# How far ahead the experts' weight tiles are requested: 43 instead of 34 before the experts' stage, 38 instead of 34 within it

## The chip, the cores and the metric

The kernel runs on one core of one Trainium2 chip. The metric is the device time of one execution in microseconds (us). The engines are PE (matrix products, with PEld for the loads of its weights), DVE and ACT (elementwise work), POOL (elementwise work and the indirect DMAs) and SP, which issues nearly all plain DMAs in one queue, strictly in order. All DMAs share 16 DMA engines.

## The reference, cut to what matters

The program is one decoder block over 1024 tokens of width 1024: adaLN modulation, a projection to q, k and v, eight heads of dilated window attention and eight of stick-breaking attention, the output projection with the residual, and then a mixture of 32 SwiGLU experts, of which each token takes two of one group of eight. The part around the change is the mixture:

```
order = jnp.argsort(expert)
...
buf = jnp.zeros((cap, d), h.dtype).at[dest].set(h[tok_sorted])
...
return (jax.nn.silu(xb @ w_gate[e]) * (xb @ w_up[e])) @ w_down[e]
...
contrib = y[dest] * w_sorted[:, None].astype(y.dtype)
return jnp.zeros((n, d), y.dtype).at[tok_sorted].add(contrib)
```

After it come the second residual and a last RMSNorm. All is float32. An expert's weights are 6 MB (1024x512 for the gate, the same for the up projection, 512x1024 down), so 32 experts bring 201 MB through the DMA engines.

## The kernel before, in words

**Slots.** All large tiles (inputs, scores, weights, intermediate results) live in one pool `u` of `NSLOT = 49` slots of 128 partitions x 4 KB. A new tile takes a slot that an earlier tile has given back in the order of the program; if the earlier tile's last reader or writer, a DMA among them, is not done when the new tile is first written, the writer waits. Which slot a tile gets is settled when the program is built.

**Order.** The whole program is unrolled and every engine runs its instructions in the order in which they were recorded. In the attention's last pair of heads the recorded order weaves three strands together: the attention itself, the output projection with the residual (`out_mm`), and the routing (`route0` to `route3`), tile of 128 tokens by tile. Into this the requests for the experts' weights are spread by `load_to(n)`, which requests weight tiles until `n` have been requested in all:

```
def spread(us, mark, to):
    m = len(us) - mark
    for j in range(m, 0, -1):
        us.insert(mark + j, p0(lambda c=held[0] + (to - held[0]) * j // m: load_to(c)))
    held[0] = to
```

`LDS` gives the number reached after each of the eight token tiles (and two steps behind them). Such a request waits for the ACT instruction recorded just before it, and from the 15th on for the landing of the request 14 before (`PACE`). The requests stand in SP's queue between the loads of `x` (L118, `x<-acc`) and its stores (L936, `x1d<-x`), on which the routing and the gathers rest.

**The experts' stage.** Twelve tiles of 512 KB make an expert's weights: `ew_0` to `ew_7` for gate and up, `ew_8` to `ew_11` for down. Ahead of each product the loop requests more, so that the requests stand `LL` tiles beyond the product:

```
if kind in "GD":
    load_to(max(loaded[0], wpos[o] + LL - wpos[o] * LT // len(wseq)))
```

Each expert e goes through these steps: POOL gathers its tokens' rows into `xe` (L1222), ACT scales them (L1233), PE transposes them into `xp` (L1255) and ACT and DVE write `xs`; PE multiplies by the gate and up tiles into `gu` (L1266, L1273); ACT and DVE make `act`; PE transposes it into `ap` (L1306) and ACT copies that into the tile `at` (L1308, step T); PE multiplies `at` by the down tiles into `y` (step D); ACT and DVE make `ys` (step Y), and POOL adds its rows into `acc` in DRAM by an indirect DMA (L1339), called the scatter here. The tile `ys` can give its slot to another only when its scatter has landed. Experts 0 to 4 and the even ones above hold up to 96 tokens, the odd ones from 5 on 64, so from expert 4 on the work repeats in pairs of one large and one small expert, with 24 weight tiles each. Recorded order around a step T: the first four or five gate and up products of the next expert, T, one more of these products, then D and Y of the expert, then the rest of the next one's. Tile `xs`, `act`, `sg`, `at`, `yt` and `ys` take their slots from the same pool as the weights.

Of the kernel before, what the change touches and what calls it, by code (L numbers as in the profile page):

```python
# [38 lines left out]
RP, RU = 6, 0  # L39
PO = 1  # L40
PO2 = 22
LDS = [6, 6, 11, 14, 18, 22, 28, 33, 33, 34]
PACE = 14
TZ, DZ = 2, 3
NG, NP = 12, 3
# [14 lines left out]
QS = "AS"  # L60
TAIL = "s3 s4 s5 r0-3 o0 y o1 g3-6 o2 s6 s7 x o3 o4 g6-9 o5 o6 o7 o8"
XA, TA, DA = 6, 4, 5
LLX = 34
LT = 0
NT = 0
PLO = ()
# [30 lines left out]
def build(nc, tc, I, out, cap=CAP):  # L97
# [944 lines left out]

    LOADS = LDS

# [176 lines left out]
    def load_x(e):  # L1221
        g = G.indirect_dma_start(out=XE[e % 3][:capof(e)], out_offset=None, in_=x1d[:],  # L1222
                                 in_offset=bass.IndirectOffsetOnAxis(ap=listof(e), axis=0),
                                 bounds_check=T - 1, oob_is_err=False)
        if e == 1:
            after[0] = g.ins
# [146 lines left out]

    LL = LLX
    load_x(0)
# [209 lines left out]
```

## Time and profile before

| | us |
|---|---|
| median of 3 runs | 1330.21 (1327.76 to 1332.28) |
| profiled execution, its own time | 1326.88 |
| its span, first to last instruction | 1325.1 |
| PE busy in the span | 1161.6 |
| first product of the experts' stage | 741.8 |
| last `at` copy (expert 31) | 1278.9 |

The profiled execution is 3.3 us below the median, and 1.8 us of it lie outside the span. The page's busy shares are averages over stages that are limited by different things: up to 740 us PE and DVE alternate, and the DMA engines have idle time; from 740 us on they are nearly always busy. So the experts' stage is read by itself, by its rhythm: the time from one small expert's `at` copy to the next small expert's, which covers one pair.

### The profile page before, as it was taken

The numbers are of one execution on the slowest core, as the hardware profiler recorded it, in microseconds if no ns is written. First come the engines' busy times: TensorE is split into PE (matmuls) and PEld (weight loads), VectorE is DVE, ScalarE is ACT, GpSimd is POOL, SyncE is SP. The second block draws the span as 40 slices with busy tenths as digits, with TensorE's granted clock in tenths as the row PEclk, the third lists the DMA queues.
The fourth block names the chain that finished last, engine by engine and source line by source line (L and its number), as shares of the span: only waits on it lengthen the run. The fifth ranks groups of instructions, "written<-read, shape, count | busy, mean of one in ns | idle before, by whom it ended". The sixth has DMA issues, their size and how long they took to land.

```text
span 1325.1 us, 19365 instructions
## 1 busy us (share of the span) xinstructions
PE 1161.6 (88%) x6800; PEld 685.0 (52%) x6800; DVE 736.3 (56%) x1418; ACT 531.2 (40%) x1079; POOL 239.7 (18%) x306
## 2 busy tenths in 40 slices
PE   4699999999999999699887999899999998899960
PEld 3497778778866887477666422232332222222310
DVE  6958773865497848978866243333333333333324
ACT  5246553656555435434534432332222222222212
POOL 3600010110100002322323111111111111111203
PEclk9799999999999999899999899999999999999985
DMA  9423443431001010356667899999999999999984
GB/s 354 166 67 97 155 149 105 145 74 55 22 27 48 17 65 0 132 209 237 244 223 260 301 319 363 358 384 376 374 373 377 370 376 378 377 380 391 361 287 196
DMA packets 89384, 304.54 MB, mean 230 GB/s; under 512 B 12417, under 2 KB 14849, under 8 KB 89282
## 3 DMA queue, kind: packets, MB, share of 16 engines
q1 hardware_dynamic: 81778, 282.00, 57.6%
q0 software_dynamic: 6352, 17.05, 5.4%
q10 hardware_dynamic: 1152, 4.19, 0.8%
q8 instruction: 56, 0.92, 0.3%
q14 instruction: 46, 0.38, 0.1%
HBM read 278.30 MB, written 29.63 MB: 232 GB/s over the span
## 4 chain that ended last, share of the span: by engine, by line
PE 44%; DVE 22%; DMA 19%; ACT 8%; issue 4%; POOL 2%; SPq 0%; POOLq 0%; DVEq 0%; ACTq 0%
DMA ew<-we 16%; PE y L1266 5%; PE gu L1266 5%; PE o L573 4%; DVE K L532 3%; DVE wada L210 2%; PE tp L549 2%; PE op L666 2%; PE op L668 2%; PE op L667 2%; PE y L1273 2%; DVE P L514 2%; PE gu L1273 2%; PE pv L460 2%; PE pj L417 2%
## 5 line engine op out<-in xcount | busy, mean ns | idle before, releaser
L1266 PE MATMUL gu<-ew,xs 128*64 128x512 f32 x1024 | 249.0, 606 | 9.2 <-DMA ew<-we 5.7
L1324 DVE TENSOR_TENSOR ys<-y,bc_gate 64x512 f32<-64x512 f32 x64 | 44.0, 688 | 215.3 <-PE y L1273 128.5
L1266 PEld LDWEIGHTS gu<-ew,xs 128*64 128x64 f32 x1024 | 63.2, 136 | 142.7 <-issue 78.1
L1266 PE MATMUL y<-ew,at 128*64 128x512 f32 x512 | 124.4, 614 | 11.1 <-DMA ew<-we 8.8
L1243 ACT ACTIVATE xs<-xp,modc,affn 128x96 f32<-128x96 f32 (+1 forms) x128 | 51.6, 418 | 155.0 <-PE xp L1255 92.7
L1339 POOL DMA_INDIRECT acc<-ys,lsP x27 | 38.7, 1434 | 372.8 <-DVE ys L1330 230.8
L549 PE MATMUL tp<-ident,P 128*128 128x128 f32 x576 | 88.5, 279 | 18.9 <-DVE P L533 11.2
L532 DVE TENSOR_TENSOR_SCAN K<-K 128x1024 f32<-128x1024 f32 (+7 forms) x64 | 92.9, 1451 | 5.9 <-ACT K L520 5.7
L516 ACT ACTIVATE P<-P,st 128x1024 f32<-128x1024 f32 (+7 forms) x64 | 49.8, 778 | 87.9 <-DVE st L529 45.4
L549 PEld LDWEIGHTS tp<-ident,P 128*128 128x128 f32 x576 | 65.5, 141 | 37.1 <-DVE P L533 9.7
L573 PE MATMUL o<-PT,v 128*64 128x256 f32 (+1 forms) x640 | 75.5, 375 | 9.4 <-DVE PT L554 5.8
L1266 PEld LDWEIGHTS y<-ew,at 128*64 128x64 f32 x512 | 34.8, 138 | 93.5 <-issue 41.8
L1241 DVE TENSOR_SCALAR xs<-xp,affn,modc 128x96 f32<-128x96 f32 (+1 forms) x128 | 45.4, 363 | 61.1 <-ACT xs L1243 56.7
L520 ACT ACTIVATE K<-S 128x1024 f32<-128x1024 f32 (+7 forms) x64 | 41.8, 653 | 71.4 <-PE S L503 34.1
L210 DVE CUSTOM_DVE_ANT_0 wada<-wada,sc 128x1024 f32<-128x1024 f32 x48 | 64.4, 1353 | 9.7 <-DMA wada<-w_adaT 9.6
L1273 PE MATMUL gu<-ew,xs 128*32 128x512 f32 x576 | 69.3, 598 | 0.0
L514 DVE CUSTOM_DVE_ANT_0 P<-S,B 128x1024 f32<-128x1024 f32 (+7 forms) x64 | 48.3, 755 | 35.8 <-PE S L501 32.9
L1278 ACT ACTIVATE yt<-y 64x512 f32<-64x512 f32 x18 | 10.7, 593 | 141.4 <-PE xp L1255 119.6
L573 PEld LDWEIGHTS o<-PT,v 128*64 128x64 f32 x640 | 46.2, 141 | 39.4 <-DVE PT L554 8.3
L552 ACT ACTIVATE PT<-tp 128x512 f32<-128x512 f32 (+3 forms) x120 | 56.0, 494 | 14.9 <-PE tp L549 14.0
L533 DVE TENSOR_TENSOR P<-P,K 128x1023 f32<-128x1023 f32 (+7 forms) x64 | 51.6, 806 | 5.7 <-ACT P L521 0.7
L554 DVE COPY PT<-tp 128x512 f32<-128x512 f32 (+3 forms) x72 | 37.3, 537 | 16.1 <-PE tp L549 15.7
(632 smaller groups left out, 2510.4 us busy)
## 6 DMA issues: line engine op xcount, KB each, us to landing
ew<-we SPq DMA_DIRECT2D x384, 512.0 KB
wada<-w_adaT SPq DMA_DIRECT2D x48, 512.0 KB
wqk<-wqk SPq DMA_DIRECT2D x16, 512.0 KB
xT<-xT SPq DMA_DIRECT2D x16, 256.0 KB
wv<-wv SPq DMA_DIRECT2D x8, 512.0 KB
B<-bias SPq DMA_DIRECT2D x8, 512.0 KB
wo<-w_out SPq DMA_DIRECT2D x8, 512.0 KB
x<-x SPq DMA_DIRECT2D x8, 512.0 KB
```

Of the source, the lines that this page charges most:

```text
L210: V.tensor_tensor_reduce(w, w, sc, op0=ALU.mult, op1=ALU.add, scale=1.0, scalar=0.0, accum_out=modc[:, v * 8 + k:v * 8 + k + 1])
L514: V.tensor_tensor_reduce(e, s, Bt[p, hd][:, :L], op0=ALU.add, op1=ALU.min, scale=-0.125, scalar=BIG, accum_out=st[:, 0:1])
L516: A.activation(e, e, AF.Exp, bias=st[:, 0:1], scale=-1.0, accum_out=st[:, 2:3])
L532: V.tensor_tensor_scan(k[:, :L], k[:, :L], k[:, :L], 1.0, op0=ALU.mult, op1=ALU.bypass)
L533: V.tensor_mul(b[:, 1:L], b[:, 1:L], k[:, 0:L - 1])
L549: PE.transpose(tp[:, jl - 4 * x, :], e[:, (jl - qo) * 128:(jl - qo) * 128 + 128], ident)
L552: A.activation(dst, tp[:, j0 - 4 * x:j1 - 4 * x, :], AF.Copy)
L573: PE.matmul(ps[hd * 64:hd * 64 + 64, 0:w], VV[p][:, j, hd * 64:hd * 64 + 64], pt[hd][jl // 4][:, jl % 4, 0:w], start=(n == 0), stop=(n == ...
L1241: V.tensor_scalar(dst, src, affn[:, k:k + 1], modc[:, 24 + k:25 + k], op0=ALU.mult, op1=ALU.add)
L1243: A.activation(dst, src, AF.Identity, scale=affn[:, k:k + 1], bias=modc[:, 24 + k:25 + k])
L1266: PE.matmul(ps[h * 64:h * 64 + 64, 0:512], a[:, i, 0:64], w[:, h * 512:h * 512 + 512], start=(i == 0), stop=(i == n - 1))
L1273: PE.matmul(ps[r:r + 32, 512:1024], a[:, j, 64:96], w[:, h * 512:h * 512 + 512], start=(j < 2), stop=(j >= n - 2))
```

## The change

Two tables of numbers change; no instruction is added or removed, on any engine:

```diff
-LDS = [6, 6, 11, 14, 18, 22, 28, 33, 33, 34]
+LDS = [12, 12, 15, 18, 22, 25, 31, 39, 42, 43]
...
-LLX = 34
+LLX = 38
```

After the first token tile's work 12 weight tiles have been requested instead of 6, and 43 instead of 34 when the routing ends. In the experts' stage the first six products request nothing new, and from then on requests stand 38 tiles ahead instead of 34.

The first place is SP's queue at the start of the last pair's requests (`x` is the residual tile of 128 tokens, the number behind it names the token tile; `ew` are weight tiles). Before:

```order
142 L936 DMA x1d<-x_6_5523 128x1024
143 L976 DMA ew_3_5632<-we 128x1024
144 L976 DMA ew_4_5634<-we 128x1024
145 L976 DMA ew_5_5636<-we 128x1024
146 L118 DMA x_4_5652<-acc 128x1024
147 L936 DMA x1d<-x_7_5525 128x1024
148 L118 DMA x_5_5838<-acc 128x1024
149 L976 DMA ew_6_5840<-we 128x1024
```

And now, in the same part of SP's queue:

```order
142 L976 DMA ew_3_5612<-we 128x1024
143 L976 DMA ew_4_5614<-we 128x1024
144 L976 DMA ew_5_5616<-we 128x1024
145 L936 DMA x1d<-x_6_5523 128x1024
146 L976 DMA ew_6_5638<-we 128x1024
147 L976 DMA ew_7_5640<-we 128x1024
148 L976 DMA ew_0_5642<-we 128x1024
149 L976 DMA ew_1_5644<-we 128x1024
150 L976 DMA ew_2_5646<-we 128x1024
151 L976 DMA ew_3_5648<-we 128x1024
152 L118 DMA x_4_5664<-acc 128x1024
153 L936 DMA x1d<-x_7_5525 128x1024
```

Three weight requests have moved ahead of the store of `x_6`, and six stand between it and the load of `x_4`, where three stood.

On ACT, PE, DVE and POOL the order of the instructions is unchanged; what the tables move there is which slot a tile gets and so what its first writer waits for. The second place is ACT at step T of the small experts 5 and 7, with the counters that each instruction waits for (DMAHW counts landings of plain DMAs, DMASW those of POOL's indirect DMAs, PE and DVE are those engines' own progress). Before:

```order
743 L1233 ACTIVATE xe_6760<-xe_6760,wlP 64x1024 [waits DMASW3_49]
744 L1291 ACTIVATE sg_7740<-gu_7633 64x512 [waits DMAHW7_49,DMAHW5_49,PE_49]
745 L1308 ACTIVATE at_7783<-ap_7778 128x256 [waits DMAHW2_49,PE_49]
...
759 L1291 ACTIVATE sg_7972<-gu_7865 64x512 [waits DMAHW5_49,DMAHW4_49,PE_49]
760 L1308 ACTIVATE at_8015<-ap_8010 128x256 [waits DMAHW4_49,DMAHW2_49,PE_49]
```

And now:

```order
743 L1233 ACTIVATE xe_6772<-xe_6772,wlP 64x1024 [waits DMASW3_49,Activation_49]
744 L1291 ACTIVATE sg_7757<-gu_7650 64x512 [waits DMAHW2_49,DMAHW0_49,PE_49]
745 L1308 ACTIVATE at_7791<-ap_7786 128x256 [waits DMAHW5_49,DMASW4_49,PE_49]
...
759 L1291 ACTIVATE sg_7989<-gu_7882 64x512 [waits DMAHW7_49,DMAHW0_49,PE_49]
760 L1308 ACTIVATE at_8023<-ap_8018 128x256 [waits DMASW0_49,PE_49]
```

The `at` copies of experts 5 and 7 have gained a wait for an indirect DMA, DMASW4 and DMASW0, and so have those of all odd experts up to 27, with these two counters in turn. Which DMA that is, POOL's order in the changed program tells (scatters and gathers from expert 4 on; each scatter waits for the one before it, since both add into `acc`):

```order
215 L1339 DMA acc<-ys_7701,lsP 1024x1024 [waits DMASW2_49,DVE_49]
216 L1222 DMA xe_6774<-x1d,lsP 96x1024 [waits DMASW5_49,PE_49,Activation_49]
217 L1339 DMA acc<-ys_7814,lsP 1024x1024 [waits DMASW4_49,DVE_49]
218 L1222 DMA xe_6770<-x1d,lsP 64x1024 [waits DMASW7_49,PE_49,Activation_49]
219 L1339 DMA acc<-ys_7933,lsP 1024x1024 [waits DMASW6_49,DVE_49]
220 L1222 DMA xe_6772<-x1d,lsP 96x1024 [waits DMASW1_49,PE_49,Activation_49]
221 L1339 DMA acc<-ys_8046,lsP 1024x1024 [waits DMASW0_49,DVE_49]
```

`ys_7701` is expert 4's and `ys_7814` expert 5's: expert 5's scatter waits on DMASW4 for expert 4's, and expert 7's on DMASW0 for expert 6's. So `at` of a small expert now waits for the landing of the scatter of the large expert just before it, whose slot it has been given.

## Rows read from the trace of the kernel before

**Rows 1.** The page: DMA share in 40 slices; chain by engine and by line
```profile
DMA  9423443431001010356667899999999999999984
...
PE 44%; DVE 22%; DMA 19%; ACT 8%; issue 4%; POOL 2%; SPq 0%; POOLq 0%; DVEq 0%; ACTq 0%
```

**Rows 2.** Stretches of the experts' stage: start:end, length, busy us, clock, DMA share, GB/s
```profile
740.00:851.00 111.00, 104.17 (x626) 32.51 (x624) 41.04 (x75) 34.88 (x62) 13.12 (x11) 0.99 0.97 350
851.00:1069.00 218.00, 207.82 (x1181) 66.29 (x1177) 79.30 (x147) 64.15 (x119) 33.76 (x28) 1.00 1.02 374
1069.00:1249.00 180.00, 160.28 (x852) 45.75 (x848) 56.79 (x105) 46.21 (x86) 27.45 (x27) 0.98 1.02 380
```

**Rows 3.** ACT's timeline, the at copies of experts 5, 7, 19 and 29: start, length
```profile
851.55 0.38 ACT L1308 ACTIVATE at<-ap 128x256 f32<-128x256 f32 x1 [1.82 <-PE ap L1306]
...
882.67 0.38 ACT L1308 ACTIVATE at<-ap 128x256 f32<-128x256 f32 x1 [1.81 <-PE ap L1306]
...
1069.46 0.38 ACT L1308 ACTIVATE at<-ap 128x256 f32<-128x256 f32 x1 [1.82 <-PE ap L1306]
...
1248.61 0.38 ACT L1308 ACTIVATE at<-ap 128x256 f32<-128x256 f32 x1 [1.92 <-PE ap L1306]
```

**Rows 4.** Waits of PE and PEld, 1070 to 1249 us: total us, times, longest
```profile
PEld y L1266 <- DMA ew<-we: 31.4, 25, 3.3
...
PE y L1266 <- DMA ew<-we: 8.8, 9, 2.4
```

**Rows 5.** Groups of PE, 851 to 1069 us: after the second bar, idle time before them
```profile
L1266 PE MATMUL gu<-ew,xs 128*64 128x512 f32 x448 | 108.1, 603 | 1.4 <-DVE xs L1241 1.4
L1266 PE MATMUL y<-ew,at 128*64 128x512 f32 x224 | 50.4, 592 | 0.0
...
L1306 PE MATMUL ap<-ident,act 64*128 64x64 f32 (+1 forms) x57 | 7.3, 248 | 8.7 <-DVE act L1298 8.7
```

**Rows 6.** POOL's timeline at expert 4's scatter
```profile
846.29 1.42 POOL L1339 DMA_INDIRECT acc<-ys,lsP  x1 [16.54 <-DVE ys L1330]
```

**Rows 7.** Line 1339 from 846 to 848 us, the same scatter: issue to landing
```profile
DMA to landing us min/median/max: 8.2/8.2/8.2
```

**Rows 8.** Line 1339 from 1032 to 1035 us, expert 16's scatter
```profile
DMA to landing us min/median/max: 8.6/8.6/8.6
```

**Rows 9.** Line 1339 from 970 to 973 us, expert 12's scatter
```profile
DMA to landing us min/median/max: 8.0/8.0/8.0
```

**Rows 10.** Line 1339 over the whole span, all 31 scatters
```profile
DMA to landing us min/median/max: 5.7/7.4/8.8
```

**Rows 11.** PE's timeline at expert 5's step T and first down product
```profile
851.05 0.46 PE L1306 MATMUL ap<-ident,act 64*128 64x64 f32 x4
851.44 1.08 PE L1266 MATMUL gu<-ew,xs 128*64 128x512 f32 x4
852.35 1.03 PE L1266 MATMUL y<-ew,at 128*64 128x512 f32 x4
```

**Rows 12.** Requests of weight tiles in 605 to 730 us: count, first and last start
```profile
L976 SPq DMA_DIRECT2D ew<-we x34: 327/330/1279, 610.0 to 727.7; - x34
```

**Rows 13.** The same in 730 to 742 us
```profile
L976 SPq DMA_DIRECT2D ew<-we x7: 328/369/511, 735.3 to 738.5; - x7
```

**Rows 14.** SP's own waits, 742 to 851 us: total us, times, longest
```profile
SPq L976 <- PE gu L1273: 28.1, 9, 7.5
SPq L976 <- PE y L1273: 20.7, 9, 5.0
SPq L976 <- DMA acc<-ys,ls: 14.9, 4, 4.3
```

**Rows 15.** SP's timeline around the load of token tile 4
```profile
621.36 1.28 SPq L976 DMA_DIRECT2D ew<-we  x3
622.69 0.42 SPq L118 DMA_DIRECT2D x<-acc  x1
```

**Rows 16.** DVE's timeline: first use of token tile 4; first use of expert 0's rows
```profile
639.38 0.75 DVE L671 SCALAR_TENSOR_TENSOR x<-op,r_out,x 128x512 f32<-128x512 f32 x1
...
733.41 0.55 DVE L1236 TENSOR_SCALAR xe<-xe,lacc 96x640 f32<-96x640 f32 x1 [0.45 <-DMA xe<-x1d,ls]
```

**Rows 17.** PE's timeline at the start of the experts' stage
```profile
740.40 1.22 PE L1255 MATMUL xp<-ident,xe 96*128 96x96 f32 x8
741.77 0.65 PE L1266 MATMUL gu<-ew,xs 128*64 128x512 f32 x2
```

## The prediction, written before the changed kernel ran

> **What bounds the kernel now.** I read the slices first, then stretches of the experts' stage, then its rhythm on ACT, then waits. In the slices the reader is to see that the DMA engines have idle time until slice 22 and none to speak of from there to the end of the experts' stage; the chain gives PE 44% and DMA 19% of the span [rows 1]. An average over the stage would call it DMA-bound. The three stretches say more [rows 2]: DMA share 0.97, 1.02 and 1.02, but PE is busy 207.8 of 218 us in the middle one and only 160.3 of 180 in the last. So PE sets the pace first and runs into the stream of weights later.
>
> The rhythm shows where. Each of the `at` copies named here belongs to a small expert, and a pair of experts lies between two odd ones [rows 3]. From expert 5 to 7 it takes 882.67 - 851.55 = 31.12 us; from 5 to 19 (seven pairs) 217.91, again 31.13 a pair; from 19 to 29 (five pairs) 179.15, or 35.8. PE's own pace is thus 31.13 us a pair, and at it expert 29 would come at 851.55 + 12 x 31.13 = 1225.1. It comes at 1248.61: 23.5 us late. The waits of that stretch name the cause, PE and its weight loads waiting for `ew` [rows 4]; in the stretch before, PE waits next to nothing for weights, and the largest idle time ahead of a group is 8.7 us over seven pairs [rows 5]. In the last stretch 120 tiles take 179.15 us, 1.49 us a tile; this is the price of a tile when the stream is full. The weights requested ahead are spent by expert 19, and 23.5 us is all that a better stream could give back before expert 29.
>
> **The change part by part.** It adds and removes no instruction. It moves requests, and with them slots.
>
> Requests before the stage: 34 by 727.7 us now [rows 12], then seven more at 735.3 to 738.5 [rows 13], 41 ahead of the first product at 741.77 [rows 17]. The change has 43 by the end of the routing; the next needs a slot that the first expert's products give back, as the 42nd does now. So not nine tiles are gained, but two, 2 x 1.49 = 3.0 us of stream, because seven of the nine already come in the gap before the first product.
>
> Requests in the stage: 38 instead of 34 ahead. Between 742 and 851 us SP waits for slots (28.1, 20.7 and 14.9 us, for products and scatters) [rows 14], yet the DMA engines are 0.97 busy there; filling the rest gives 0.03 x 111 = 3.3 us. Together the stream ends 3 to 6 us earlier (four tiles of depth are 6.0 us).
>
> What these requests pass: the loads of `x` in SP's queue. The tightest is token tile 4: its load starts at 622.69 behind three weights [rows 15] and is first used at 639.38 [rows 16], 16.7 us on. The change puts six weights ahead of it: 3 x 1.49 = 4.5 us, and 3 x 0.43 = 1.3 us of issue. With the slowest landing of any scatter, 8.8 us [rows 10], as a high estimate for such a load, it is there after 14.6 us. I take nothing, and up to 2 us if the load is slower; the cover is DVE's other work. The gathers of the first experts' rows meet more weights in flight: expert 0's rows are used at 733.41 as they land [rows 16], and PE transposes them at 740.40 [rows 17]; ACT's and PE's work in between (the gate row, the warm-up products) covers about 6 us. I take nothing, at most 2 us.
>
> The added wait. `at` of each odd expert from 5 to 27, twelve of them, now waits for the scatter of the large expert ahead. Expert 4's scatter is issued at 846.29 [rows 6] and lands 8.2 us later [rows 7], at 854.5; `at` of expert 5 runs at 851.55, 5.26 us after the issue. It will start 8.2 - 5.26 = 2.9 us late. Behind it on ACT stands nothing that PE needs sooner; on PE stand the four down products, and everything after them. PE does one more gate product from 851.44 and starts the down products at 852.35 [rows 11], 0.42 us after `at` ends (851.93), so this much is covered, less some 0.04 for the signal. Cost for PE: 2.9 - 0.4 = 2.5 us. Other scatters of large experts land after 8.6 us [rows 8] and 8.0 [rows 9]; six whose time the view tells give 8.2, 8.1, 8.0, 8.6, 8.0, 8.1, mean 8.17. I take 8.17 - 5.26 - 0.38 = 2.53 us for each, since the order ahead of `at` is unchanged and the queue is as full as now. Twelve are 30.4 us. From both sides: with the median of all 31 landings, small experts' among them, 7.4 us [rows 10], it is 1.76 each and 21.1; with the longest, 8.8 us, 3.16 and 37.9. Experts 1 to 3 have such waits too, but a large expert's `at` comes later behind the scatter; nothing.
>
> The Trainium skill speaks here, in the page Perfetto Trace Analysis, section Identifying Performance Opportunities: the same gap again and again on an engine that should be saturated can mean that there is no room in SBUF for the next tile. The trace agrees so far that no such gap recurs while the slots suffice: the groups of the middle stretch show 1.4 and 8.7 us of idle time over seven pairs [rows 5]. By that rule a change that takes more slots for weights would be recognised by a new gap, once a pair.
>
> The sum. PE's pace becomes 31.13 + 2.53 = 33.7 us a pair. This is slower than now where PE sets the pace and faster than the 35.8 of the end: PE no longer overtakes the stream, so the 23.5 us of waiting go, and 30.4 us of stalls come. Net +6.9 us. The stream isn't in the way: it delivers as now or 3 to 6 us sooner, and PE comes 7 us later. Against the profiled execution (span 1325.1, own time 1326.88) that is 1333.8; the median of the runs, 1330.21, stands 3.3 us above it, so I forecast 1337.1.
>
> **The rivals.** *Earlier requests win (faster).* If the wait of `at` is already over when it comes, by a scatter landing in under 5.6 us, the stream alone decides and the time falls by 3 to 6 us, to 1324 to 1327. For it: the shortest landing is 5.7 us [rows 10]. Against it: the large experts' scatters show 8.0 to 8.6. The Trainium skill's page DMA: Bandwidth & Descriptors, section Rules for kernel authors, advises to issue a DMA early, compute, and wait late, so that its cost overlaps. By that rule this rival is what happens; the rows on the middle stretch, where DMA share is 1.02, differ, because an earlier request there only queues longer.
>
> *Both cancel (no change).* At the median landing, 7.4 us, 21.1 us of stalls stand against 23.5 of waiting: -2.4 us, 1327.8. It needs scatters 0.8 us shorter than those measured. The point from which stalls outweigh is 23.5 / 12 = 1.96 us each, a landing of 7.6 us.
>
> *The clock falls behind each stall (slower by far).* In the last stretch, with PE idle for a tenth of the time, the granted clock was 0.98 instead of 1.00 [rows 2]: 0.02 x 180 = 3.6 us. That much again would make the sum +10.5. If each of the twelve stalls cost its own length once more in a spell at 1.2 instead of 2.4 GHz, 2.5 us, it would be +37, 1367. Against it: much idle time in the last stretch left the clock at 0.98.
>
> *The requests hold up the routing (slower).* If the loads of `x` land late, the experts' stage starts later; 2 us for one tile, at most 8 over all tiles, on top of the sum: up to 1345.
>
> **How the numbers follow.** The forecast, stalls a little above what is won back: 0.62; its own range is 1332 (2.1 us a stall, a landing after 7.7 us, net +1.8) to 1348 (37.9 us of stalls, net +14.4, and 3.6 us of clock). Earlier requests win: 0.15. Cancelling: 0.13. Clock: 0.05. Routing: 0.05. The range from 1325 to 1349 leaves out half of the first rival, most of the clock's and little else. A measurement of this kernel tells about 0.3%, 4 us, from no change. Faster: two thirds of the first rival and a little of the second, 0.13. Slower: 0.54 of the forecast's 0.62, the clock and the routing, 0.64. Within: the rest, 0.23.
>
> **What would show it.** Right: ACT's `at` rows of odd experts 5 to 27 show idle time ended by the scatter (`acc<-ys`), some 2.5 us more than now, and PE waits before the first down product of small experts; the pairs take 33.5 to 34 us evenly from expert 5 to 29; the waits for `ew` after 1069 us have nearly gone; weight requests number 43 by about 730 us, and the next starts with the first expert's products at about 746. The first product stays at 742 within 2 us. Wrong: pairs of 31 us (no stall), or stalls together with waits for weights late in the stage (then the two add up and the time passes 1349), or a stage that starts later than 744.

## The result, and the profile after

The changed kernel takes 1350.24 us (median of 4 runs, 1344.57 to 1352.38) against 1331.24 for the kernel before on the same chip: ratio 1.0132, 95% interval 1.0107 to 1.0157. It is slower by 14 to 21 us. The forecast was slower, 1337; the median lies 1.2 us above the upper end of the range, 1349. So the loss is 19.0 us where 6.9 was forecast, nearly three times as much. The profiled execution took 1349.15 us with a span of 1347.4, so its span is 22.3 us longer than before's 1325.1.

The rhythm comes first: ACT's timeline at the `at` copies of experts 5, 7, 19 and 29 in the changed kernel (start, length; in brackets ACT's idle time ahead of the row and what ended it).

```profile
858.68 0.38 ACT L1308 ACTIVATE at<-ap 128x256 f32<-128x256 f32 x1 [5.63 <-issue]
...
892.39 0.38 ACT L1308 ACTIVATE at<-ap 128x256 f32<-128x256 f32 x1 [4.72 <-DMA acc<-ys,lsP]
...
1099.34 0.38 ACT L1308 ACTIVATE at<-ap 128x256 f32<-128x256 f32 x1 [4.57 <-DMA acc<-ys,lsP]
...
1271.35 0.38 ACT L1308 ACTIVATE at<-ap 128x256 f32<-128x256 f32 x1 [1.93 <-PE ap L1306]
```

Before, ACT idled 1.8 us here and PE's transposes ended it [rows 3]. Now it idles 4.6 to 5.6, and the scatter ends it (for expert 5 the profile names no releaser, but the scatter's landing, below, meets it). From expert 5 to 7 the pair takes 33.71 us instead of 31.12. Expert 29, which has no such wait, is back at 1.93.

On PE the same stall stands between two rows of its timeline, expert 7:

```profile
888.99 0.46 PE L1306 MATMUL ap<-ident,act 64*128 64x64 f32 x4
889.38 1.08 PE L1266 MATMUL gu<-ew,xs 128*64 128x512 f32 x4
892.83 3.65 PE L1266 MATMUL y<-ew,at 128*64 128x512 f32 x16 [2.37 <-ACT at L1308]
```

Before, the down products of expert 5 followed the gate product without a gap [rows 11]. Over the whole span the page's group of the down products adds the stalls up (busy, mean ns, idle time ahead of them); 30.8 us of the 31.3 are the twelve stalls of experts 5 to 27, 2.21 to 3.28 us each:

```profile
L1266 PE MATMUL y<-ew,at 128*64 128x512 f32 x512 | 128.1, 647 | 31.3 <-ACT at L1308 31.3
```

The scatter of expert 4 on POOL, and its issue to landing, answer to [rows 6, 7]; under it the landing over all scatters [rows 10]:

```profile
849.61 1.42 POOL L1339 DMA_INDIRECT acc<-ys,lsP  x1 [18.18 <-DVE ys L1330]
```

```profile
DMA to landing us min/median/max: 9.0/9.0/9.0
...
DMA to landing us min/median/max: 4.6/7.9/9.0
```

It lands at 858.6 and `at` starts at 858.68. In the stretch from 1070 to 1249 us the waits for `ew` that headed the list of PE and PEld before [rows 4] are gone from the top; in their place stand

```profile
PEld y L1266 <- ACT at L1308: 19.5, 10, 3.9
...
PE y L1266 <- ACT at L1308: 12.9, 5, 3.1
```

The idle time of line 1266's products (PE and PEld together) from 1070 to 1249 that ended with a weight's landing was 51.7 us, in 48 pieces, before; it is now

```profile
  DMA ew<-we: 12.7, 31
```

The three stretches of the stage (columns as in [rows 2]):

```profile
740.00:851.00 111.00, 104.13 (x631) 33.69 (x631) 40.03 (x73) 34.07 (x62) 12.10 (x10) 0.98 0.94 330
851.00:1069.00 218.00, 191.32 (x1054) 59.59 (x1052) 69.48 (x129) 57.40 (x106) 29.95 (x26) 0.98 1.02 377
1069.00:1249.00 180.00, 159.89 (x876) 49.85 (x876) 59.06 (x111) 47.50 (x90) 26.52 (x22) 0.97 1.02 379
```

PE lost 16.5 us of work in the middle stretch, where it had run almost without a break. And there is something the sum had not counted: the granted clock is 0.98 and 0.97 where it was 1.00 and 0.98. Between the two levels, 1.2 and 2.4 GHz, a mean of c stands for 2 x (1 - c) of the time at the lower one: 8.7 + 10.8 = 19.5 us here, 7.2 before. Slices of 1 us, in which rounding matters less, give 20.5 and 6.8. One such spell, behind expert 11's stall (the short stretch as a window, then PE's timeline):

```profile
959.80:963.20 3.40, 3.08 (x8) 1.01 (x10) 0.00 (x0) 0.27 (x1) 0.00 (x0) 0.51 1.00 307
```

```profile
956.78 1.08 PE L1266 MATMUL gu<-ew,xs 128*64 128x512 f32 x4
960.12 5.19 PE L1266 MATMUL y<-ew,at 128*64 128x512 f32 x16 [2.26 <-ACT at L1308]
```

The same 16 products that took 3.65 us behind expert 7's stall take 5.19 here, because the clock had fallen while PE stood still: in slices of 0.4 us it is 0.50 from 960.0 on, ahead of their start at 960.12. The other rows of this kind stand behind the stalls of experts 17, 19, 23 and 25:

```profile
1063.43 6.43 PE L1266 MATMUL y<-ew,at 128*64 128x512 f32 x16 [2.98 <-ACT at L1308]
...
1099.78 5.33 PE L1266 MATMUL y<-ew,at 128*64 128x512 f32 x16 [2.22 <-ACT at L1308]
...
1170.11 5.35 PE L1266 MATMUL y<-ew,at 128*64 128x512 f32 x16 [3.06 <-ACT at L1308]
...
1205.37 5.35 PE L1266 MATMUL y<-ew,at 128*64 128x512 f32 x16 [2.21 <-ACT at L1308]
```

Against 3.65 us each, the five rows are 9.4 us longer in all. Behind the other seven stalls the products take 3.65.

Where the 22.3 us lie, from the `at` rows of both traces: 1.70 ahead of expert 0 (759.71 and 761.41), 5.43 from expert 0 to 5, 15.61 from 5 to 29 (397.06 and 412.67), 1.45 from 29 to 31, and 1.89 less behind it. The first of the twelve stalls delays expert 5's own copy, so the stretch from 5 to 29 holds eleven of them.

Requests, SP's line 976 in the changed kernel, from 605 to 730, 730 to 735 and 735 to 752 us (the first of the second row is the last of the first):

```profile
L976 SPq DMA_DIRECT2D ew<-we x40: 327/379/1391, 613.6 to 729.9; - x40
...
L976 SPq DMA_DIRECT2D ew<-we x4: 527/596/761, 729.9 to 732.1; - x4
...
L976 SPq DMA_DIRECT2D ew<-we x2: 328/342/356, 748.1 to 749.5; - x2
```

43 by 732.1, the next with the first products, as forecast. Expert 0's rows were scaled late, and the first product hardly was:

```profile
740.78 0.55 DVE L1236 TENSOR_SCALAR xe<-xe,lacc 96x640 f32<-96x640 f32 x1 [4.91 <-DMA xe<-x1d,ls]
...
743.42 1.94 PE L1266 MATMUL gu<-ew,xs 128*64 128x512 f32 x8 [0.19 <-ACT xs L1243]
```

733.41 became 740.78 [rows 16], 7.4 us; 741.77 became 743.42 [rows 17], 1.65 us. Such a difference says little: in the eleven profiled executions expert 0's `at` copy (in the runs that keep it in `act`'s slot, the copy there) comes between 756.6 and 765.1 us, and before, the run with the wait alone and the one with dummies in the kernel before, whose recorded order is the same up to there, have 759.7, 765.1 and 756.6.

### The profile page after: what moved, and what is told of

It is laid out like the page before. It is cut to its first block, busy times and chain, and to the rows that moved or that the text cites. A ratio compares the mean times of both kernels' runs of the same rounds, so it can differ in the third digit from the quotient of the medians.

```text
span 1347.4 us, 19379 instructions
## 1 busy us (share of the span) xinstructions
PE 1164.4 (86%) x6800; PEld 689.6 (51%) x6800; DVE 736.0 (55%) x1418; ACT 531.4 (39%) x1079; POOL 240.5 (18%) x306
## 5 line engine op out<-in xcount | busy, mean ns | idle before, releaser
L1266 PE MATMUL y<-ew,at 128*64 128x512 f32 x512 | 128.1, 647 | 31.3 <-ACT at L1308 31.3
L1266 PEld LDWEIGHTS y<-ew,at 128*64 128x64 f32 x512 | 38.4, 149 | 117.5 <-issue 53.2
L573 PE MATMUL o<-PT,v 128*64 128x256 f32 (+1 forms) x640 | 71.5, 363 | 9.7 <-DVE PT L554 4.8
L1308 ACT ACTIVATE at<-ap 128x384 f32<-128x384 f32 (+1 forms) x32 | 14.2, 444 | 97.3 <-DMA acc<-ys,lsP 53.4
## 6 DMA issues: line engine op xcount, KB each, us to landing
ew<-we SPq DMA_DIRECT2D x384, 512.0 KB, 10.2
```

The source lines that it names most:

```text
L573: PE.matmul(ps[hd * 64:hd * 64 + 64, 0:w], VV[p][:, j, hd * 64:hd * 64 + 64], pt[hd][jl // 4][:, jl % 4, 0:w], start=(n == 0), stop=(n == ...
L1266: PE.matmul(ps[h * 64:h * 64 + 64, 0:512], a[:, i, 0:64], w[:, h * 512:h * 512 + 512], start=(i == 0), stop=(i == n - 1))
```

## The experiments

The theory (T): the 38th tile takes a slot that `at` needs; the stalls that follow, and the clock that falls in them, are the whole loss. Against it: R1, the early requests hold up attention or routing; R2, the clock spells have nothing to do with the gap; R3, more requests at once slow the stage. Each run was compared with the kernel before on the same chip.

### The new list alone

```diff
-LDS = [6, 6, 11, 14, 18, 22, 28, 33, 33, 34]
+LDS = [12, 12, 15, 18, 22, 25, 31, 39, 42, 43]
```

> The kernel before with the new list of requests during the last pair's attention and the routing (43 by the experts' stage), and 34 ahead of the products as before. Theory T (the 12 waits of odd experts' `at` for a scatter, and the clock that falls in them, make the kernel slower; both come from 38 ahead alone): no such wait here, the ACT rows of `at` idle some 1.8 us as before, so 1326 to 1333 us, within 0.4% of before: the stage may start 1 to 3 us later or its weights come 0 to 3 us earlier. Rival R1 (the early requests hold up the attention or the routing): most of the loss is here, 1340 us or more, and the first product of the experts' stage comes 8 us or more later.

Measured: 1331.27 us, ratio 1.0004 [0.9987, 1.0020]. The idle time of line 1266's products from 1070 to 1249 that ended with a weight's landing, 51.7 us before:

```profile
  DMA ew<-we: 51.6, 50
```

R1 falls: the early requests cost nothing that can be told. They bring nothing either.

### 38 ahead alone

```diff
-LLX = 34
+LLX = 38
```

> The kernel before with 38 tiles ahead of the products in the place of 34, and the old list of requests. Theory T: the 12 waits stand as in the changed kernel, some 2.7 us each on TensorE, the waits for weights are gone, and granted-clock spells at half come back in the experts' stage: 1343 to 1353 us (before 1331, changed kernel 1350). Rival R1 (the early requests cost it): 1328 to 1334 us, like before, whatever the waits do.

Measured: 1351.86 us, ratio 1.0172 [1.0147, 1.0198]. `at` of expert 7, and the last two stretches:

```profile
894.16 0.38 ACT L1308 ACTIVATE at<-ap 128x256 f32<-128x256 f32 x1 [5.25 <-DMA acc<-ys,lsP]
```

```profile
851.00:1069.00 218.00, 191.08 (x1032) 59.09 (x1031) 69.11 (x128) 55.50 (x103) 28.97 (x24) 0.95 1.01 372
1069.00:1249.00 180.00, 159.31 (x870) 50.04 (x872) 57.99 (x107) 46.63 (x87) 24.32 (x21) 0.97 1.02 379
```

The whole loss is in this one number. It is somewhat more than the changed kernel's 1.0132 [1.0107, 1.0157]; the two intervals overlap a little, and the traces differ in the clock: 30.7 us at the lower level from 851 to 1249 here (slices of 1 us), 20.5 there.

### The wait alone

```diff
-        A.activation(st["a"], tp, AF.Copy)
+        d = A.activation(st["a"], tp, AF.Copy)
+        if e in SMALL and 5 <= e <= 27:
+            queue_after(d, SC[e - 1])
```

(`SC[e]` is the scatter of expert e, kept where it is issued; 34 ahead and the old list stay.)

> The kernel before, all its requests as they were, with one thing added: the activation that fills `at` of the odd experts 5 to 27 also waits for the scatter of the large expert ahead of it. Theory T: the wait is the whole loss. The stalls (12 of 2.5 to 3 us, 30 to 36 in all) give the weights the same time to arrive, so the 23 us of waits for weights go, and the clock falls as in the changed kernel: 1341 to 1353 us. Rival R3 (the deeper requests, through more traffic at once, are what slows the stage or the scatters' landing): the wait without the deeper requests costs no more than it gives back, 1328 to 1337 us, and the landing of the scatters' DMAs is shorter than in the changed kernel by 1 us or more.

Measured: 1346.89 us, ratio 1.0133 [1.0116, 1.0150], like the changed kernel. The stall is there (the profile names no releaser for this added wait), and the clock:

```profile
894.47 0.38 ACT L1308 ACTIVATE at<-ap 128x256 f32<-128x256 f32 x1 [4.88 <-issue]
```

```profile
851.00:1069.00 218.00, 190.70 (x1048) 58.99 (x1044) 70.92 (x133) 58.08 (x108) 31.34 (x26) 0.98 1.02 377
1069.00:1249.00 180.00, 159.51 (x898) 50.22 (x900) 59.66 (x112) 49.14 (x92) 26.52 (x22) 1.00 1.02 378
```

R3 falls: not one request was changed. From 851 to 1250 us the scatters land after 7.9 us at the median here and after 7.7 in the changed kernel, so deeper requests don't slow them. This profiled run had only 10.2 us at the lower clock (slices of 1 us). Its pairs from 5 to 29 took 408.85 us, 3.8 less than the changed kernel's and 11.8 more than before's; its stage began 5.4 us later than before's, ahead of anything that was edited. So that the two ratios agree so closely is in part chance.

### 37 ahead, with the new list

```diff
-LLX = 38
+LLX = 37
```

(against the changed kernel)

> The changed kernel with 37 tiles ahead of the products in the place of 38, and the new list. One tile less leaves `at` a slot that is free early, so theory T has no wait for a scatter here: 1322 to 1331 us, 0 to 8 us below before (43 tiles and 3 more ahead delay the point from which weights are late), and no more half-clock spells in the experts' stage than before's three. Rival R3 (deeper requests cost by themselves): a tile less changes little, 1343 us or more.

Measured: 1333.96 us, ratio 1.0026 [1.0012, 1.0041]. `at` of experts 5 and 29, and the idle time ended by weights as above:

```profile
853.43 0.38 ACT L1308 ACTIVATE at<-ap 128x256 f32<-128x256 f32 x1 [1.82 <-PE ap L1306]
...
1252.23 0.38 ACT L1308 ACTIVATE at<-ap 128x256 f32<-128x256 f32 x1 [1.92 <-PE ap L1306]
```

```profile
  DMA ew<-we: 52.9, 46
```

One tile fewer and the stall is gone: it is the slot. The hoped-for gain isn't there; the waits for weights are as long as before, and 5 to 29 takes 398.80 us against 397.06. I had expected 1322 to 1331 and was wrong on that.

### The changed kernel with TensorE kept busy in the stall

```diff
+        if f == 0 and e in SMALL and 5 <= e <= 27:
+            warm(8)
```

(ahead of the down product's loop; it adds 32 dummy products that nothing reads)

> The changed kernel with 32 dummy products (128x128, bf16, into a tile that nothing reads) ahead of the first down product of the odd experts 5 to 27, so that TensorE works in the stall instead of standing still; the 12 waits stay. Theory T (the idle gap is what lets the clock fall, and the half-clock spells after e5 cost some 10 of the 20 us): the spells in the experts' stage go down to the three that before has, and the time to 1338 to 1344 us. Rival R2 (the spells have nothing to do with the gap; the wait alone left a run with few of them that was as slow): 1346 us or more, with as many spells as the changed kernel or as many lost us without them.

Measured: 1337.62 us, ratio 1.0046 [1.0025, 1.0067]. `at` of expert 13 on ACT, then PE's timeline around it:

```profile
989.73 0.38 ACT L1308 ACTIVATE at<-ap 128x256 f32<-128x256 f32 x1 [4.74 <-DMA acc<-ys,lsP]
```

```profile
986.69 1.08 PE L1266 MATMUL gu<-ew,xs 128*64 128x512 f32 x4
987.71 1.96 PE L263 MATMUL scr<-onesb 128*128 128x128 bf16 x32
990.17 3.65 PE L1266 MATMUL y<-ew,at 128*64 128x512 f32 x16 [0.50 <-ACT at L1308]
```

```profile
851.00:1069.00 218.00, 204.41 (x1300) 72.59 (x1301) 71.41 (x133) 58.64 (x110) 31.35 (x26) 1.00 1.02 377
1069.00:1249.00 180.00, 167.71 (x1051) 58.41 (x1047) 58.48 (x108) 47.48 (x88) 24.12 (x20) 1.00 1.02 376
```

The waits are as long as in the changed kernel, the products start as late, and the clock stays at 1.00, in each slice of 1 us from 851 to 1249. The median, 0.4 us below the range of T, falls by 12.6 us (1350.24 - 1337.62), the ratio to before by 0.86%, or 11.4 us. Not all of that is the clock: of the 12.1 us between the two profiled executions 3.7 lie ahead of expert 0 (its copy comes at 757.72 and 761.41), where the two kernels do the same. From 5 to 29, where the dummies act, it takes 404.03 us, 8.6 less than the changed kernel, and 6.97 more than before. R2 falls: with the pause filled, the clock is not lost.

### The same dummies in the kernel before

The same two lines, with 34 ahead and the old list.

> The kernel before with the same 32 dummy products at the same 12 places (some 1.96 us each on TensorE, 23.5 us in all), where there is no stall for them to fill. It is the control for the run with the dummies in the changed kernel, and a test of what bounds the kernel before. If the stream of weights sets the end of the stage there (theory), the dummies only use up the 23.5 us in which TensorE waited for weights: 1328 to 1336 us, and the waits for weights from 1070 to 1249 fall from 51.7 us to under 35. If TensorE's own work sets it, all of it shows: 1350 us or more. If the dummies make a kernel faster by something other than filling the stall, this one is faster than before too: under 1325 us.

Measured: 1330.06 us, ratio 0.9983 [0.9967, 1.0000]. The last stretch, and the idle time ended by weights:

```profile
1069.00:1249.00 180.00, 172.23 (x1080) 59.51 (x1076) 62.79 (x116) 49.66 (x92) 29.32 (x28) 1.00 1.02 376
```

```profile
  DMA ew<-we: 9.2, 18
```

12 x 1.96 = 23.5 us of useless work on PE cost nothing. The stream sets the end in the kernel before; 51.7 us of idle time became 9.2, and 5 to 29 took 399.10 us. And the dummies don't speed up a kernel that has no stall by more than a measurement can tell.

### `at` in a slot of its neighbour

```diff
-            act = st["act"] = slot(f"act{e}")[:, 0:512]
+            st["full"] = slot(f"act{e}")
+            act = st["act"] = st["full"][:, 0:512]
...
-        st["a"] = slot(f"at{e}")[:, 0:4 * c].rearrange("p (k t) -> p k t", k=4)
+        st["a"] = st.pop("full")[:, 512:512 + 4 * c].rearrange("p (k t) -> p k t", k=4)
```

> The changed kernel, with all its requests, and `at` put into the unused upper half of `act`'s slot, so that it takes no slot and waits for no scatter. Theory T: the stalls and the extra clock spells go, and waits for weights come back as in before, since the run with 37 ahead showed that the stream's pace sets the second half whatever is asked for: 1325 to 1334 us. Rival R3 (deeper requests cost by themselves): 1340 us or more.

Measured: 1330.62 us, ratio 0.9995 [0.9980, 1.0011]. The 38 tiles and the new list are all there, and the loss is gone: one slot was the price. Idle time ended by weights, as above:

```profile
  DMA ew<-we: 49.9, 48
```

The same with 40 ahead:

> As e3_at_half with 40 tiles ahead instead of 38, and no new wait in the experts' stage. If what limits the stream from the stage's start to e5 is the number of tiles that may be under way (its DMA share there is 0.92 to 0.97 against 1.02 later), each tile more is worth up to one tile's landing, 35.8/16 = 2.2 us: 1318 to 1328 us, faster than before. If the release of slots by the products limits it, no gain: 1327 to 1335 us.

Measured: 1329.51 us, ratio 0.9983 [0.9967, 0.9999], and with the old list:

> The kernel before with `at` in `act`'s slot and 40 tiles ahead, and the old list of requests. Against e8_half40 it tells what the new list is worth when nothing else is in its way: theory T (the list moves requests that land in time anyway) within 3 us of it; if the early requests hold something up (the run with the new list alone was level with before), it is 3 us or more below it: 1318 to 1326 us.

Measured: 1329.80 us, ratio 0.9990 [0.9974, 1.0005]. The first is the best version by its interval, but by 0.17%, less than the 0.3% that a measurement tells from no change; the two lists agree within 0.3 us. The three stretches with 40 ahead and the new list, and its idle time ended by weights:

```profile
740.00:851.00 111.00, 104.09 (x633) 34.99 (x634) 40.04 (x73) 34.11 (x62) 12.11 (x10) 0.98 0.93 329
851.00:1069.00 218.00, 207.44 (x1176) 66.12 (x1174) 79.04 (x147) 64.23 (x119) 33.50 (x29) 1.00 1.01 373
1069.00:1249.00 180.00, 159.94 (x862) 45.73 (x862) 57.70 (x108) 47.95 (x88) 26.98 (x26) 0.99 1.02 380
```

```profile
  DMA ew<-we: 52.1, 49
```

My upper hope of 2.2 us a tile came from a slip (a pair has 24 tiles, 1.49 us each), but even by that six tiles would be 9 us, and they brought nothing that can be told.

## Why the prediction was right, and where its size was off

**The added wait: right in place and size.** Stalls of 2.53 us on PE, 30.4 us in twelve, were forecast from the landing of 8.17 us. The twelve measure 30.8 us, where the middle stretch had 0.0 before [rows 5]. In the run with the clock held up, where nothing else is in the way, the pair from 5 to 7 takes 33.66 us; the forecast was 33.7. All twelve pairs there take 404.03 / 12 = 33.67 us, but that mean agrees by luck: eleven with the stall take 33.66 to 34.95, and the last, without one, 30.91. In the changed kernel the pairs are not even, as the prediction had them, but 33.6 to 36.35, since some hold slow products. The run with the wait alone and the one with 37 ahead show that this wait, and the slot behind it, is the cause.

**What is given back: right.** The waits for weights late in the stage went (51.7 us of idle time became 12.7), and stalls and waits don't add up: PE no longer overtakes the stream. The dummies in the kernel before show the same from the other side. Stalls less waits, forecast at +6.9 us, is what the run with the clock held up measures: 0.46% of 1331.5, 6.1 us, interval 3.3 to 8.9.

**The clock: the term that was mis-sized.** The sum took it as nothing and the prediction gave the rival 0.05, because "much idle time in the last stretch left the clock at 0.98". It measured 9.4 us in the changed kernel's own trace, where the down products behind five of the twelve stalls are that much longer, and 8.6 us from expert 5 to 29 between the profiled runs without and with the dummies. Three kernels with the stall show price and clock together: with 10.2, 20.5 and 30.7 us at the lower clock (the wait alone, the changed kernel, 38 ahead alone) the stretch from 5 to 29 takes 4.8, 8.6 and 12.6 us more than with the dummies and none. The 12.6 us between the medians hold some 4 us more than that, which the spread from run to run covers (the changed kernel's four runs go from 1344.57 to 1352.38). So 6.1 us of stalls less waits and some 9 us of clock are shown of the 19.0; the rest is not told apart from that spread. The rival's two prices, 3.6 us and one more length of all stalls (30 us), bracket it, but its chance rested on a wrong reading. In the kernel before, a lost clock cost next to nothing, since the stream was the limit: PE had 23.5 us to spare there, as the dummies show. Now PE sets the pace, and every slow product counts. It may matter too, and no run isolates it, that PE waited in shorter pieces before (PEld's mean 31.4 / 25 = 1.3 us [rows 4]), while each new stall leaves it idle for 2.2 to 3.3 us at once. Behind expert 11's stall the down products take 5.19 us for 3.65. The Trainium skill, TensorE: Matmul & The Clock Gate, section A second HAM failure mode: psum-queue depth-cycling, reports of another kernel that short idle times of TensorE between groups of products, when they come often enough, make its clock swing between the two levels, and that the throughput falls by what throttling and warming up again cost between the bursts. The trace agrees: the clock is 0.98 and 0.97 with the pauses and 1.00 in the run where they were filled. This rule, weighed as a rival with a larger chance, would have moved the forecast toward the result.

**Requests and stream: counted right as not binding, and worth nothing.** 43 tiles by 732.1 us, and the next at 748.1. "3 to 6 us earlier" was too much, and is not to be seen in any time: the list alone is 1.0004, 37 ahead 1.0026, 40 ahead without any stall 0.9983. The DMA share of the middle stretch was 1.02 already. With 40 ahead that stretch moves 373 GB/s, against 374 before; filling the queue deeper doesn't make it faster. Ahead of that stretch the greater depth is hardly used: by 851 us SP had requested 108 weight tiles before and 109 in the changed kernel and in both runs with 40 ahead, and from 742 to 851 us it waits for slots, with 40 ahead and the new list 27.6 us for the gate and up products of line 1273 and 20.6 for scatters (28.1 and 14.9 before [rows 14]). That fits the second reading in the expectation for 40 ahead, that the release of slots is the limit; no run isolates it.

**Routing and start of the stage: right.** The first product came at 743.42, inside the 2 us named. Expert 0's rows, used 7.4 us later, were covered but for 1.65 us, and the list alone costs nothing that can be told.

**The rival of earlier requests, and the cancelling one: wrong in their premise.** They needed landings under 5.6 or near 7.4 us; the large experts' took 7.9 to 9.0 from expert 4 on. The shorter ones, 7.1 to 7.5, are the small experts'.

Open: why some stalls lower the clock and others don't. Their length doesn't tell: in the changed kernel the longest, expert 5's 3.28 us, does not, and expert 25's 2.21 us does; and three profiled runs with the same waits have 10.2, 20.5 and 30.7 us at the lower clock. Open too is the DMA share of 0.93 before expert 5 with 40 ahead. It goes with the list, 0.91 to 0.94 in all six runs with the new one and 0.96 to 0.99 in the five with the old; that more of the first 43 tiles have then landed before 740 us is the likely reason, but it was not tried.

## What to carry to other kernels

A deeper prefetch is paid in buffers. Before raising it, find which short-lived tile gets the last free slot, and what releases that slot: if it is a DMA's landing, the wait is that landing less the time since its issue, once per iteration. If the engine that stalls is then the one that sets the pace, count a share of the stall again for its clock (here 9.4 us on 30.8), and test it by filling the gap with idle work; and once the DMA engines are full, a longer queue of requests buys no time.

## What the runs showed of the hardware that was not expected

Pauses of 2.2 to 3.3 us on TensorE, one in each pair of 33.7 us or more, went with the lower clock for 20.5 of 398 us in the changed kernel, and for 30.7 in the run with 38 ahead alone. 32 dummy products of 1.96 us in all, in the same pause, kept the clock at 1.00 from 851 to 1249 us, though 0.4 to 1.7 us of the pause remained. So filling a stall that stayed gave back more, 8.6 us from expert 5 to 29, than the stall's own net cost of 6.1.

The scatters' landing, 7.1 to 9.0 us while weights stream, did not grow with deeper requests: the median from 851 to 1250 us is 7.3 before, 7.9 with the wait alone and the old requests, 7.7 in the changed kernel.
